# Input powers before the rotation tables and later in the block order; a fourth pooling block on unscaled input

## The chip, the cores and the metric

The kernel runs on one core of one Trainium2 chip. The core has five engines with queues of their own: TensorE (PE, matrix products into PSUM), VectorE (DVE), ScalarE (ACT), GpSimd (POOL) and SyncE (SP, which here issues nearly all DMAs). Each queue runs in order. The metric is device time of one execution in microseconds, the median over runs: 940.18 us before the change (3 runs, 939.85 to 941.1).

## The reference

A trunk of two layers over 512 tokens of width 1024, float32. Each layer normalises its input (RMSNorm), forms one wide projection of it, runs three mixers on slices of that projection, merges them by sigmoid gates, projects the sum and adds it to the residual:

```python
h = rmsnorm(x, norm_g[l])
z = h @ w_in[l]
a_val, a_gate, b_val, b_gate, c_u, c_v, c_gate, gates = jnp.split(z, split_idx, axis=-1)
ya = s5_mixer(a_val, ...) * jax.nn.silu(a_gate)
yb = pool_mixer(b_val, pool_w[l], pool_scale[l]) * jax.nn.silu(b_gate)
yc = sgu_mixer(c_u, c_v, ...) * jax.nn.silu(c_gate)
proj = einsum('blkc,kcd->blkd', stack([ya, yb, yc], 2), w_branch[l])
x = x + sum(sigmoid(gates) * proj, axis=2) @ w_out[l]
```

The s5 mixer is a diagonal complex state space: 32 groups of 16 channels with 64 states each, discretised from `lam`, `log_dt`, `b`, `c`, scanned over time, followed by GELU and a half GLU. The pool mixer takes, in four groups of channels (g = 0 to 3), the mean over a trailing window of 2, 4, 8 or 16 tokens minus the token, and maps each group by a 128x128 matrix. The third mixer (sgu) mixes positions in blocks of 128.

## The kernel before

**Blocks.** The work is a stream of blocks, each one product of a 1024x128 (or 512x128) piece of a weight matrix with the 512 tokens. Each weight and each activation is split into a rounded high part and a rest (`hi`/`lo`, `wh`/`wl`), and a step k of a product is three matmuls, hi x hi, lo x hi and hi x lo (`step`, lines 105 to 107). A block has 8 steps, a branch projection 4. SP loads the raw weights into three buffers `wr`, ACT makes `wh` (L157) and DVE makes `wl` (L158), each of three buffers, up to two blocks ahead of PE (`stream`; up to five are loaded or prepared).

**Layer 0, in PE's order.** Four value blocks for the state space, four pooling blocks (g = 3, 2, 1, 0), four pool gates (same order; each ends with a one-step product `psb` of the pooled group `pt[g]` with its split 128x128 matrix `wq[0]`), then the first merge: gate blocks `opened(m)` of 8 steps, and `joined(m)` of 4. Then the third mixer, its merge, the gates and GLU of the state space, its merge, and the output projection. Blocks before the norm is known run on the unscaled split input (`norm.hs`, tiles `gh`/`gl`) and are scaled afterwards by DVE (L739 for pooling). From the fourth value block on, `scaled()` makes the scaled input: per k a product `hf` on DVE (L675), `hi` on ACT (L677) and `lo` on DVE (L678). In `early` are the pooling groups of layer 0 that use the unscaled input: 3, 2 and 1; group 0 uses the scaled one, and ACT copies its result (L741).

**Side work.** The state space of a layer runs beside the blocks as a generator (`s5_side`). A software clock advances by 0.64 per step; in the fourth step of each product and at the end of each block a tick resumes the generator if its pause has passed. That decides where its PE instructions stand in PE's order, which is written out by hand. The order of the other engines is found by a planner at build time from its own estimate of durations; side work has lower priority there by 1000. Buffers of a pool are handed out in that planning too.

In layer 0 the generator first collects the values (`uu`), copies tables (`stacked`, on ACT), and writes `rotations`: some 150 small operations on POOL that build the tables `tlo` and `thi` from cos and sin of the discretisation. After a pause `W_POWERS` it writes `input_powers`: six DVE operations (L385, L386, L388) that make `ak` from `kre`, `kim`, `apr`, `api`, four transposes on PE (L391, `psa`), a copy on ACT (L393) and a store to DRAM (L394, `akd`). Then come four steps t: `s5_output`, `s5_input` (loads of `akd`, L457, and `bi`, L458, into buffers) and `s5_tables` (POOL, L501 to 507, from `tlo` and `thi`); after a pause (`W_PREP` for t = 0, else `W_OPS`) the lag products `psk` (L514); after `W_STATE` the state products `pse` (L550), whose results DVE multiplies with the tables at L555; after `W_OUT` the output products `psy` (L578 and L581), then GELU, a store and a gather into `ych` (L592). `outputs()` splits `ych` ahead of the GLU.

**Buffers.** `slot` is the large pool, 49 tiles of 128x512 (line 59). `spare` is a pool of six such tiles (`fp`, line 60) that the state space uses for `apr` and `api` (held until `stacked` and the powers have read them), `ai`, `bi`, `e`, `sbc` and others. `small_spare` is a pool of eight half tiles (`fs`, line 61) that holds the temporaries of the discretisation, of `rotations` (`tb`, L410) and of `input_powers` (`ak`, L384 and L387).

Of the kernel before, what the change touches and what calls it, by code (L numbers as in the profile page):

```python
# [7 lines left out]
F32 = mybir.dt.float32  # L8
# [7 lines left out]
P = 128  # L16
# [3 lines left out]
NS = 8  # L20
NK = 64
# [4 lines left out]
GELU_A = 0.044715  # L26
GELU_B = 1.5957691216057308
SIDE = 1000
W_POWERS = 32.0
W_PREP = (30.0, 25.0)  # L30
W_OPS = 15.0
W_STATE = 5.0
W_OUT = 16.0
# [19 lines left out]
def hybrid_trunk(ctx: ExitStack, tc, xT, wi, wbr, wo, wglu, wmisc, pv, rows, gain, slam, sbc, sbt, cst, out):  # L53
# [19 lines left out]
    def nm(s):  # L73
        count[0] += 1
        return f"{s}_{count[0]}"

    def slot(s="s", dt=F32, shape=(P, T)):
        return sp.tile(list(shape), dt, tag="s", name=nm(s))

    def spare(s="f", dt=F32, shape=(P, T)):  # L80
        return fp.tile(list(shape), dt, tag="f", name=nm(s))

    def small_spare(s="f", shape=(P, T // 2)):
        return fs.tile(list(shape), F32, tag="fs", name=nm(s))
# [282 lines left out]
    def stacked():  # L367
        for h in range(2):
            for r in range(2):
                a, b = slice(64 * r, 64 * r + 64), slice(64 * h, 64 * h + 64)  # L370
                for o, x, sign in ((war, apr, 1 - 2 * r), (wai, api, -1)):
                    S.activation(o[a].rearrange("p j (q h) -> p j h q", h=2)[:, :, h], x[b], AF.Copy, scale=float(sign))
                for o, x, sign in ((kar, kre, 1), (kai, kim, 2 * r - 1)):
                    S.activation(o[a].rearrange("p (q h) -> p h q", h=2)[:, h], x[b], AF.Copy, scale=float(sign))
# [63 lines left out]
    def flat(a):  # L438
        return a.rearrange("p q k -> p (q k)")
# [85 lines left out]
    def s5_side(l, ud, st):  # L525
        uu = bp.tile([P, 4, 8, NK], F32, tag="ba", name=nm("uu"))
        for s in range(NS):
            r = 16 * (NS - 1 - s)
            src = ud.rearrange("n (g c) (s k) -> s c (n g) k", c=16, s=NS)[s]
            nc.sync.dma_start(uu[r : r + 16].rearrange("p n g k -> p (n g) k"), src)  # L530
        if l == 0:
            stacked()
            rotations(*angle)
            yield W_POWERS
            input_powers()
            yield 3
        ych = bp.tile([P, 4, T], F32, tag="bb", name=nm("ych"))
        st["ych"] = ych
        for t in range(4):
            w = s5_output(l, t)  # L540
            e = s5_input(l, t)
            tcs, tsn, rt = s5_tables(l, t)
            yield W_PREP[l] if t == 0 else W_OPS
            s5_lags(l, t, w)
            yield W_STATE
            ps = pe.tile([P, 2, 4, NK], F32, tag="pe", name=nm("pse"))
            for r in range(2):
                for i in range(4):
                    for h in range(2):
                        PE.matmul(ps[64 * h : 64 * h + 64, r, i], e[r][:, 2 * i + h], uu[:, t, 2 * i + h], start=True, stop=True)  # L550
            sr, si = flat(ps[:, 0]), flat(ps[:, 1])

            def mul(x, y, eng=V):
                o = small_spare("p5")
                eng.tensor_tensor(o, x, y, ALU.mult)  # L555
                return o

            a, b = mul(sr, tcs), mul(si, tsn)
            G.tensor_tensor(a, a, b, ALU.add)  # L559
            d, c = mul(si, tcs), mul(sr, tsn)  # L560
            V.tensor_tensor(d, d, c, ALU.subtract)
            gr, gi = small_spare("g5"), small_spare("g5")
            V.tensor_tensor_scan(gr, rt, a, 0.0, ALU.mult, ALU.add)
            V.tensor_tensor_scan(gi, rt, d, 0.0, ALU.mult, ALU.add)
            b, c = mul(gi, tsn, G), mul(gr, tsn, G)
            a, d = mul(gr, tcs), mul(gi, tcs)
            v3 = lambda z: z.rearrange("p (q k) -> p q k", q=4)[:, :, 0 : NK - 1]
            for r, (x, y, op) in enumerate(((a, b, ALU.subtract), (d, c, ALU.add))):
                for h in range(2):
                    o = hst[64 * r : 64 * r + 64].rearrange("p (q h) k -> p h q k", h=2)[:, h, :, 1:NK]  # L570
                    i = slice(64 * h, 64 * h + 64)
                    V.tensor_tensor(o, v3(x)[i], v3(y)[i], op)
            yield W_OUT
            py = aux("psy")
            for g in range(8):
                for h in range(2):
                    o = py[64 * h : 64 * h + 64, g * NK : (g + 1) * NK]
                    PE.matmul(o, tm[:, g, 64 * h : 64 * h + 64], uu[:, t, g], start=True, stop=False)  # L578
                for h in range(2):
                    o = py[64 * h : 64 * h + 64, g * NK : (g + 1) * NK]  # L580
                    PE.matmul(o, w[:, g, 16 + 64 * h : 80 + 64 * h], hst[:, g], start=False, stop=True)  # L581
            sq = spare("sq")
            S.activation(sq, py, AF.Square)
            V.tensor_scalar(sq, sq, GELU_A, 1.0, ALU.mult, ALU.add)
            V.tensor_tensor(sq, sq, py, ALU.mult)
            S.activation(sq, sq, AF.Sigmoid, scale=GELU_B)
            V.tensor_tensor(sq, py, sq, ALU.mult)
            yd = dp.tile([P, T], F32, tag="yd", name=nm("yd"))
            nc.sync.dma_start(yd, sq)
            for g in range(8):  # L590
                src = yd.rearrange("(s c) (g k) -> g c s k", c=16, g=8)[g]
                nc.sync.dma_start(ych[16 * g : 16 * g + 16, t].rearrange("p (s k) -> p s k", s=NS), src)  # L592
# [45 lines left out]
    def layer(l, norm, nxt):  # L638
# [29 lines left out]
        def scaled():  # L668
            norm.spread()
            for n, ps in held:  # L670
                value(n, ps)
            held.clear()
            for k in range(8):
                t = slot("hf")
                V.scalar_tensor_tensor(t, xs[k], pcol(0, k), norm.rstd, ALU.mult, ALU.mult)  # L675
                hi, lo = slot("hi", F32R), slot("lo", F32R)
                S.activation(hi, t, AF.Copy)  # L677
                V.tensor_tensor(lo, t, hi.bitcast(F32), ALU.subtract)  # L678
                hs.append((hi, lo))
# [40 lines left out]
        wq = {}  # L720

        def small(i):
            raw = slot("wq", F32, (P, 4, P))
            nc.sync.dma_start(raw, wmisc[l, i])
            if i == 1:
                V.memset(raw[64:128, :, 0:64], 0.0)
            wq[i] = raw if i else split(raw, (P, 4, P))

        early = (3, 2, 1) if l == 0 else (3,)
        pt = [None] * 4  # L730
        yb = [None] * 4

        def pooled(g):
            def consume(ps):
                xp = bp.tile([P, NS, PAD + NK], F32, tag="xp", bufs=2, name=nm("xp"))
                G.memset(xp[:, :, 0:PAD], 0.0)
                xv = xp[:, :, PAD:].rearrange("p s (b k) -> p s b k", b=8)
                if g in early:
                    V.tensor_tensor(xv, by_block(ps), by_block(norm.rstd), ALU.mult)  # L739
                else:  # L740
                    S.activation(xv, by_block(ps), AF.Copy)  # L741
                cur = xp
                for j in range(g + 1):
                    nx = bp.tile([P, NS, PAD + NK], F32, tag="xq", bufs=2, name=nm("xq"))
                    if j < g:
                        G.memset(nx[:, :, 0:PAD], 0.0)
                    sh = 1 << j
                    if sh < NS:
                        G.tensor_tensor(nx[:, sh:NS, PAD:], cur[:, sh:NS, PAD:], cur[:, 0 : NS - sh, PAD:], ALU.add)
                        G.tensor_tensor(nx[:, 0:sh, PAD:], cur[:, 0:sh, PAD:], cur[:, NS - sh : NS, PAD - 1 : PAD - 1 + NK], ALU.add)  # L750
                    else:
                        o = PAD - sh // NS
                        G.tensor_tensor(nx[:, :, PAD:], cur[:, :, PAD:], cur[:, :, o : o + NK], ALU.add)
                    cur = nx
                t = slot("pt", F32, (P, NS, NK))
                V.scalar_tensor_tensor(t, cur[:, :, PAD:], 1.0 / (2 << g), xp[:, :, PAD:], ALU.mult, ALU.subtract)
                V.tensor_tensor(cur[:, :, PAD : PAD + 2], cur[:, :, PAD : PAD + 2], rcnt[:, g], ALU.mult)
                V.tensor_tensor(t[:, :, 0:2], cur[:, :, PAD : PAD + 2], xp[:, :, PAD : PAD + 2], ALU.subtract)
                pt[g] = split_steps(flat(t))
                if g == 3:  # L760
                    small(0)

            return consume
# [395 lines left out]
```

## Time and profile before

| | us |
|---|---|
| median of 3 runs | 940.18 |
| profiled execution | 941.43 |
| its span | 939.6 |
| PE busy | 882.9 (94%) |
| DVE busy | 578.1 (62%) |
| ACT busy | 299.9 (32%) |
| POOL busy | 216.0 (23%) |
| chain that ended last | PE 86%, DVE 6%, POOL 3%, DMA 2% |

The rows below are from one profiled execution. Times are from the start of its span. A wait names the operation whose end released the waiting one. Busy time of PE counts a matmul from its start to its modelled end. PEclk is the share of PE's clock that was granted; it has two levels, 1.2 and 2.4 GHz, and a value between them is a mean over a window.

### The profile page before, as it was taken

What the parts mean: (1) busy time and instruction counts of PE and PEld (TensorE: products, weight loads), DVE (VectorE), ACT (ScalarE), POOL (GpSimd) and SP (SyncE); (2) the same over time, 40 slices, a digit from 0 to 9 for tenths busy, and PEclk for the clock granted to TensorE, in tenths of its full rate; (3) what the DMA queues carried; (4) which work ended last, traced back from release to release, by engine and by line L of the source; (5) the groups of instructions that cost most, each with busy time, mean ns of one, the idle gap of its engine ahead of it and who ended that gap; (6) DMA issues with size and microseconds to landing.
All of it is one profiled execution on the core that took longest, in us unless ns stands there. A gap on an engine that the chain in (4) does not pass through costs nothing.

```text
span 939.6 us, 12276 instructions
## 1 busy us (share of the span) xinstructions
PE 882.9 (94%) x4652; PEld 719.5 (77%) x4652; DVE 578.1 (62%) x934; ACT 299.9 (32%) x440; POOL 216.0 (23%) x353
## 2 busy tenths in 40 slices
PE   9981199999999999999999999999999999999996
PEld 5861188888788878888888788887888888888885
DVE  8895173578867767444546787647884435544632
ACT  5334022322322225333433333231322223433521
POOL 1446940203233330000131730201321111000020
PEclk9986599999999999999999999999999999999998
DMA  7831033363425344223323824454432332322402
GB/s 241 168 103 45 12 90 105 121 197 119 133 80 160 92 145 146 78 92 112 112 92 135 144 72 132 142 167 140 140 101 90 92 110 82 109 91 91 156 23 89
DMA packets 65706, 106.89 MB, mean 114 GB/s; under 512 B 30176, under 2 KB 32864, under 8 KB 65648
## 3 DMA queue, kind: packets, MB, share of 16 engines
q1 hardware_dynamic: 65008, 104.88, 37.7%
q0 software_dynamic: 352, 1.10, 0.4%
q8 instruction: 36, 0.59, 0.3%
q14 instruction: 22, 0.18, 0.1%
q10 hardware_dynamic: 288, 0.14, 0.0%
HBM read 99.01 MB, written 7.08 MB: 113 GB/s over the span
## 4 chain that ended last, share of the span: by engine, by line
PE 86%; DVE 6%; POOL 3%; DMA 2%; issue 2%; ACT 1%; SPq 0%; DVEq 0%; ACTq 0%
PE mm L105 24%; PE mm L106 24%; PE mm L107 24%; PE mm L1024 2%; PE mm L1025 2%; PE mm L1026 2%; PE mm L843 1%; PE mm L844 1%; PE mm L845 1%; DVE wl L158 1%; POOL k L233 1%; PE pse L550 1%; DVE hf L675 1%; PE psy L578 1%; PE psz L865 1%
## 5 line engine op out<-in xcount | busy, mean ns | idle before, releaser
L105 PE MATMUL mm<-hi,wh 128*128 128x512 f32 x960 | 380.3, 396 | 2.8 <-ACT hi L677 2.8
L106 PE MATMUL mm<-lo,wh 128*128 128x512 f32 x960 | 376.7, 392 | 1.5 <-DVE lo L678 1.4
L107 PE MATMUL mm<-hi,wl 128*128 128x512 f32 x960 | 375.6, 391 | 1.3 <-DVE wl L158 1.3
L157 ACT ACTIVATE wh<-wr 128x1024 fp32r<-128x1024 f32 (+1 forms) x174 | 160.3, 922 | 448.5 <-PE mm L106 274.2
L158 DVE TENSOR_TENSOR wl<-wr,wh 128x1024 fp32r<-128x1024 f32 (+1 forms) x174 | 198.4, 1141 | 159.8 <-ACT wh L157 159.2
L105 PEld LDWEIGHTS mm<-hi,wh 128*128 128x128 f32 x960 | 181.5, 189 | 44.3 <-ACT hi L677 4.5
L106 PEld LDWEIGHTS mm<-lo,wh 128*128 128x128 f32 x960 | 181.5, 189 | 40.7 <-DVE lo L678 3.3
L107 PEld LDWEIGHTS mm<-hi,wl 128*128 128x128 f32 x960 | 181.5, 189 | 39.7 <-DVE wl L158 1.7
L799 DVE TENSOR_TENSOR sg<-sg,mm 128x512 f32<-128x512 f32 x48 | 32.8, 684 | 41.9 <-PE mm L107 41.9
L801 POOL TENSOR_TENSOR sg<-sg,sg 128x512 f32<-128x512 f32 x16 | 26.3, 1643 | 101.1 <-DVE sg L799 101.1
L614 POOL TENSOR_TENSOR sq<-sq,sq 128x512 f32<-128x512 f32 x7 | 12.7, 1813 | 125.0 <-ACT sq L608 114.1
L105 PE MATMUL mm<-gh,wh 128*128 128x512 f32 x96 | 38.4, 400 | 0.1
L107 PE MATMUL mm<-gh,wl 128*128 128x512 f32 x96 | 37.8, 393 | 0.4 <-DVE wl L163 0.4
L106 PE MATMUL mm<-gl,wh 128*128 128x512 f32 x96 | 37.7, 393 | 0.2 <-DVE gl L604 0.2
L391 PE MATMUL psa<-cs,ak 128*128 128x128 f32 x4 | 1.4, 447 | 38.8 <-DVE ak L388 38.8
L559 POOL TENSOR_TENSOR p<-p,p 128x256 f32<-128x256 f32 x8 | 5.9, 736 | 125.8 <-DVE p L555 125.8
L391 PEld LDWEIGHTS psa<-cs,ak 128*128 128x128 f32 x4 | 0.6, 202 | 39.6 <-DVE ak L388 39.6
L95 ACT ACTIVATE hi<-sg 128x512 fp32r<-128x512 f32 x32 | 20.2, 631 | 24.4 <-DVE sg L801 13.5
L790 ACT ACTIVATE sg<-mm 128x512 f32<-128x512 f32 x48 | 27.9, 581 | 0.0
L843 PE MATMUL mm<-wh,hi 128*128 128x512 f32 x64 | 25.4, 397 | 1.2 <-DVE sg L799 1.2
L844 PE MATMUL mm<-wl,hi 128*128 128x512 f32 x64 | 25.1, 392 | 0.9 <-DVE wl L158 0.9
L96 DVE TENSOR_TENSOR lo<-sg,hi 128x512 fp32r<-128x512 f32 x32 | 22.2, 695 | 5.9 <-ACT hi L95 5.7
(207 smaller groups left out, 1035.9 us busy)
## 6 DMA issues: line engine op xcount, KB each, us to landing
wr<-in_wi SPq DMA_DIRECT2D x102, 512.0 KB
wr<-in_wbr SPq DMA_DIRECT2D x48, 256.0 KB
wr<-in_wo SPq DMA_DIRECT2D x16, 512.0 KB
ai<-akd SPq DMA_DIRECT2D x16, 256.0 KB
bi<-in_sbt SPq DMA_DIRECT2D x16, 256.0 KB
x<-in_xT SPq DMA_DIRECT2D x8, 256.0 KB
ud<-u SPq DMA_DIRECT2D x8, 256.0 KB
uu<-ud SPq DMA_DIRECT2D x16, 128.0 KB
```

The costliest lines, as they stand in the source:

```text
L95: S.activation(hi, src, AF.Copy)
L96: V.tensor_tensor(lo, src, hi.bitcast(F32), ALU.subtract)
L105: PE.matmul(ps, whi[:, k], x[0], start=k == 0, stop=False)
L106: PE.matmul(ps, whi[:, k], x[1], start=False, stop=False)
L107: PE.matmul(ps, wlo[:, k], x[0], start=False, stop=k == n - 1)
L157: S.activation(hi, raw, AF.Copy)
L158: V.tensor_tensor(lo, raw, hi.bitcast(F32), ALU.subtract)
L790: S.activation(sg[m], ps, AF.Sigmoid)
L799: V.tensor_tensor(g, g, ps, ALU.mult)
L801: (V if last is not None else G).tensor_tensor(g, g, macc[m], ALU.add)
L843: PE.matmul(ps, th, w(wh), start=j == 0 and k == 0, stop=False)
L844: PE.matmul(ps, th, w(wl), start=False, stop=False)
```

## The change

Five edits. In `s5_side` of layer 0 the pause `W_POWERS` now comes ahead of `stacked`, `input_powers` and `rotations`, is 50 in place of 32, and the powers are written ahead of the tables. The pause before the lag products of step 0 is 25 in place of 30 in layer 0 (25 in layer 1, as before). `hf` (both layers) and `pt` are taken from the six spares in place of the large pool, and so is the raw tile of the pooling weights. The pooling block of group 0 in layer 0 runs on the unscaled input and is scaled by DVE.

```diff
--- before.py
+++ after.py
@@ -26,8 +26,8 @@
 GELU_A = 0.044715
 GELU_B = 1.5957691216057308
 SIDE = 1000
-W_POWERS = 32.0
-W_PREP = (30.0, 25.0)
+W_POWERS = 50.0
+W_PREP = (25.0, 25.0)
 W_OPS = 15.0
 W_STATE = 5.0
 W_OUT = 16.0
@@ -529,10 +529,10 @@
             src = ud.rearrange("n (g c) (s k) -> s c (n g) k", c=16, s=NS)[s]
             nc.sync.dma_start(uu[r : r + 16].rearrange("p n g k -> p (n g) k"), src)
         if l == 0:
+            yield W_POWERS
             stacked()
+            input_powers()
             rotations(*angle)
-            yield W_POWERS
-            input_powers()
             yield 3
         ych = bp.tile([P, 4, T], F32, tag="bb", name=nm("ych"))
         st["ych"] = ych
@@ -671,7 +671,7 @@
                 value(n, ps)
             held.clear()
             for k in range(8):
-                t = slot("hf")
+                t = spare("hf")
                 V.scalar_tensor_tensor(t, xs[k], pcol(0, k), norm.rstd, ALU.mult, ALU.mult)
                 hi, lo = slot("hi", F32R), slot("lo", F32R)
                 S.activation(hi, t, AF.Copy)
@@ -720,13 +720,13 @@
         wq = {}
 
         def small(i):
-            raw = slot("wq", F32, (P, 4, P))
+            raw = slot("wq", F32, (P, 4, P)) if i else spare("wq", F32, (P, 4, P))
             nc.sync.dma_start(raw, wmisc[l, i])
             if i == 1:
                 V.memset(raw[64:128, :, 0:64], 0.0)
             wq[i] = raw if i else split(raw, (P, 4, P))
 
-        early = (3, 2, 1) if l == 0 else (3,)
+        early = (3, 2, 1, 0) if l == 0 else (3,)
         pt = [None] * 4
         yb = [None] * 4
 
@@ -752,7 +752,7 @@
                         o = PAD - sh // NS
                         G.tensor_tensor(nx[:, :, PAD:], cur[:, :, PAD:], cur[:, :, o : o + NK], ALU.add)
                     cur = nx
-                t = slot("pt", F32, (P, NS, NK))
+                t = spare("pt", F32, (P, NS, NK))
                 V.scalar_tensor_tensor(t, cur[:, :, PAD:], 1.0 / (2 << g), xp[:, :, PAD:], ALU.mult, ALU.subtract)
                 V.tensor_tensor(cur[:, :, PAD : PAD + 2], cur[:, :, PAD : PAD + 2], rcnt[:, g], ALU.mult)
                 V.tensor_tensor(t[:, :, 0:2], cur[:, :, PAD : PAD + 2], xp[:, :, PAD : PAD + 2], ALU.subtract)
```

## Rows read from the trace of the kernel before

**Rows 1.** The page, part 1: busy us, share of the span, instructions

```profile
PE 882.9 (94%) x4652; PEld 719.5 (77%) x4652; DVE 578.1 (62%) x934; ACT 299.9 (32%) x440; POOL 216.0 (23%) x353
```

**Rows 2.** Waits of PE, 0 to 120 us: total us, times, longest

```profile
PE psa L391 <- DVE ak L388: 38.8, 2, 38.2
...
PE mm L105 <- ACT hi L677: 1.8, 3, 0.6
```

**Rows 3.** Timeline of PE: start, us, engine, line, operation, [idle before <- releaser]

```profile
48.77 0.39 PE L105 MATMUL mm<-hi,wh 128*128 128x512 f32 x1
...
67.35 0.39 PE L105 MATMUL psb<-hi,hi 128*128 128x512 f32 x1
...
73.47 0.39 PE L105 MATMUL psb<-hi,hi 128*128 128x512 f32 x1
...
113.76 0.69 PE L391 MATMUL psa<-cs,ak 128*128 128x128 f32 x2 [0.54 <-DVE ak L388]
...
114.10 0.78 PE L105 MATMUL mm<-hi,wh 128*128 128x512 f32 x1
...
119.21 0.40 PE L105 MATMUL mm<-hi,wh 128*128 128x512 f32 x1
```

**Rows 4.** Windows: length, busy of PE, PEld, DVE, ACT, POOL; PEclk, DMA, GB/s

```profile
53.00:64.40 11.40, 8.94 (x21) 5.74 (x22) 11.18 (x29) 4.55 (x7) 4.62 (x8) 0.70 0.40 135
...
112.00:119.20 7.20, 6.13 (x16) 4.63 (x17) 4.12 (x9) 1.02 (x2) 6.79 (x20) 0.51 0.15 43
```

**Rows 5.** Timeline of DVE, around the powers

```profile
65.46 0.68 DVE L96 TENSOR_TENSOR lo<-wq,hi 128x512 fp32r<-128x512 f32 x1
...
80.71 0.23 DVE L364 TENSOR_TENSOR kim<-k,inv 128x32 f32<-128x32 f32 x1
...
110.96 0.53 DVE L385 TENSOR_TENSOR ak<-kre,apr 128x256 f32<-128x256 f32 x1 [22.03 <-POOL thi L413]
```

**Rows 6.** Windows, the stretch of the last pooling block and two gates

```profile
48.77:74.20 25.43, 22.58 (x79) 16.17 (x77) 25.04 (x71) 8.93 (x13) 10.47 (x18) 0.87 0.28 94
```

**Rows 7.** Timeline of POOL, the rotation tables

```profile
77.81 0.93 POOL L233 TENSOR_TENSOR k<-k 128x32 f32<-128x32 f32 x2
...
90.90 0.26 POOL L411 TENSOR_TENSOR tb<-tlo,k 128x32 f32<-128x32 f32 x1
...
125.63 1.88 POOL L503 TENSOR_TENSOR tp<-tp,tp 128x256 f32<-128x256 f32 x2
```

**Rows 8.** Windows: POOL's tables in all, and one group of them twice

```profile
77.81:127.51 49.70, 14.44 (x53) 11.47 (x54) 17.64 (x37) 10.51 (x25) 46.27 (x159) 0.59 0.14 43
...
98.61:103.86 5.25, 0.00 (x0) 0.00 (x0) 0.00 (x0) 0.00 (x0) 4.92 (x18) 0.50 0.00 0
...
113.42:120.82 7.40, 7.06 (x21) 5.66 (x22) 4.35 (x10) 1.02 (x2) 7.07 (x19) 0.62 0.31 76
```

**Rows 9.** Timeline of DVE, state step 0

```profile
163.63 1.42 DVE L555 TENSOR_TENSOR p<-pse,tp 128x256 f32<-128x256 f32 x4 [1.79 <-PE pse L550]
...
167.99 1.22 DVE L158 TENSOR_TENSOR wl<-wr,wh 128x512 fp32r<-128x512 f32 x1
```

**Rows 10.** Timeline of DVE, first and last of the 16 that prepare step 0

```profile
113.62 0.34 DVE L478 TENSOR_TENSOR bt<-sbc,kar 128x128 f32<-128x128 f32 x1
...
131.59 0.68 DVE L467 TENSOR_TENSOR bi<-bi,bi 128x512 f32<-128x512 f32 x1
```

**Rows 11.** Timelines of PE, SP and ACT, end of step 3 in layer 0

```profile
325.51 0.34 PE L578 MATMUL psy<-uu,tm 128*64 128x64 f32 x4
...
339.69 0.43 SPq L592 DMA_DIRECT2D ych<-yd  x1
...
362.40 0.67 ACT L932 ACTIVATE sg<-mm,pvt 128x512 f32<-128x512 f32 x1
```

**Rows 12.** Waits of SP's issue queue: total us, times, longest

```profile
SPq L394 <- ACT ak L393: 37.1, 1, 37.1
...
SPq L457 <- DVE bpad L481: 13.0, 3, 4.5
```

## The prediction

> **What bounds the kernel now.** I read the page's busy times first: TensorE (PE) is busy for 882.9 of 939.6 us, so outside its own work only some 57 us can be won [rows 1]. The waits of PE in the first 120 us say where most of that lies: 38.8 us at line 391, the transposes of the input powers `ak`, and 1.8 us on `hi`, the scaled input [rows 2]. The timeline of PE gives their places. Three matmuls, one step k, take 0.68 us there: the nine steps between the two pool-gate products at 67.35 and 73.47 take 6.12. The second product ends at 73.47 + 0.68 = 74.15, and the next block starts at 114.10 [rows 3]. The granted clock says that a wait costs more than itself: after the 38 us it was 0.51 of full speed, the lower level of 1.2 GHz, until 119.2, and after the short waits on `hi` the stretch from 53.0 to 64.4 had 0.70 [rows 4].
>
> Why `ak` was late stands on VectorE (DVE) and GpSimd (POOL). `kim`, the last input of the powers, was done at 80.94. The first `ak` started at 110.96, after 22.03 us of idleness that ended with POOL's `thi` at line 413 [rows 5]. It reads nothing of `thi`: it needs a buffer of the small pool, eight of them, which the rotation tables, written ahead of it in the program, were passing through. POOL worked on those tables from 77.81, and on what is built from them until 127.51 [rows 7]. So a DVE job of 2.8 us (110.96 to the last transposes at 113.76) stood behind POOL's long chain of small operations. That is the wait that ends last in this stage.
>
> **The change part by part.**
> *The powers ahead of the tables.* The six `ak` operations now take their buffers first; DVE can run them when `kim` is there. No work is added. The PE position moves as well: by the block clock (0.64 per step) the first pause of 50 ends at the tick in the second gate block of the first merge, instead of behind the second pool gate. Between the two lie pool gate 1 (9 steps), pool gate 0 (9), one gate block (8) and half of another (4): 30 x 0.68 = 20.4 us of PE work that now come first. Gone is the wait, 114.10 - 74.15 = 39.95 us, less 0.25 for the four transposes themselves, and the half clock behind it: the twelve matmuls from 114.10 to 119.21 took 5.1 us where 12 x 0.227 = 2.7 is usual. A = 39.7 + 2.4 = 42.1 us.
>
> *The fourth pooling block on unscaled input.* Scaled input is then first wanted by the pool gates, one block of 8 x 0.68 = 5.44 us later. From 48.77, where the last pooling block starts, to 67.35 there are 16 steps, 10.88 us; it took 18.58. B is at most 18.58 - 10.88 = 7.7 us, waits and clock together. It is nothing if DVE doesn't get ahead: from 48.8 to 74.2 DVE was busy for 25.0 of 25.4 us [rows 6], and the low half of the pooling weights was ready at 65.46 + 0.68 = 66.14 for a product at 67.35, 1.2 us of margin [rows 3, 5]. A PE that comes 7.7 us earlier meets that. For a gain speaks that the eight `hf`, the four `pt` and the raw pooling weights no longer queue for the buffers which the unscaled input holds, so the planner may load and split the weights sooner. Added is one DVE operation of 0.7 us in place of one on ScalarE. I take B = 4, the middle of 0 to 7.7.
>
> *Where `ak` is then late.* PE would reach the transposes at 74.15 - 4 + 20.4 = 90.5 us. DVE had `kim` at 80.94; to this come the `ak` at 2.8, the weight split of 1.2 for the block that PE now runs on, and up to three gates' products and splits at some 2.0 each (three operations of 0.68), 6: 90.9. Lower bound 0 (DVE orders the powers first), upper bound 8 us (B full, PE there at 86.9, all of DVE's rest in front, and the half clock behind the wait). I take C = 1.5, near the 90.9. On SyncE the store of `akd` held the weight loads queued behind it for 37.1 us of issue time [rows 12]; that shrinks with the wait.
>
> *The tables and the shorter pauses.* This is what the old wait hid. Step 0 of the state space now starts 30 steps later on PE, but its first matmuls on the state come sooner behind the transposes: 35.84 on the block clock instead of 42.24. 35.84 x 0.68 / 0.64 = 38.1, with 1.5 for the small matmuls: DVE reaches line 555 at about 92 + 39.5 = 131.5 and needs POOL's tables there. Before, they were done at 127.51 and line 555 started at 163.63, 36 us of margin [rows 7, 9]. POOL slows beside DVE: the same group of table work took 5.25 us with DVE idle and 7.40 with DVE busy for 4.35 of them, a loss of half of DVE's time [rows 8]. The 17.64 us of DVE time in POOL's 49.70 cost 8.7, so alone it is 41.0. After the change DVE has, from 78 to 131, some 26 us of operations with both inputs in SBUF: weight splits 6 x 1.2 and 5 x 0.68 (10.6), `ak` 2.8, the preparation of step 0 (16 operations, 113.62 to 132.27, some 10) [rows 10], gate splits 2.7. At half, 13 us: tables at 77.8 + 41 + 13 = 131.8, level with DVE. The chain of 4.4 us behind line 555, until the next weight split at 167.99 [rows 9], passed before without a wait of PE; with two blocks prepared ahead, 8 us less the split itself, 1.6 us of wait on DVE are free. I take D = 1 for a start of the tables a little late, bounds 0 and 14 (R1).
>
> The Trainium skill (SBUF — State Buffer, Who interferes with whom) has a harsher rule: between GpSimd and a VectorE operation with two SBUF inputs the shared port is an exclusive lock, and the loser blocks fully. By it the group in rows 8 would have taken 5.25 + 4.35 = 9.6 us; the trace shows 7.40. By the rule POOL alone needs 32.1 and the 26 us count whole: tables at 136, PE 5 us later in place of 1, in all 901.
>
> *The end of step 3.* The last output product of layer 0 moves by 240.64 - 230.40 = 10.24 on the block clock, 10.9 us. Before, it started at 325.51, its last gather was issued by 340.12 (14.6 later), and the first GLU result was read at 362.40, so that block of 2.7 us started at 359.7 [rows 11]. 325.5 + 10.9 + 14.6, up to 4 for the gather to land and 1.3 to split: 356.3 against 359.7. Cost 0, upper bound 3.
>
> The sum: 42.1 + 4 - 1.5 - 1 = 43.6 us. The profiled execution took 941.43 us (span 939.6 and 1.8 around it), the median is 940.18, 1.25 lower. 941.43 - 43.6 - 1.25 = 896.6, so 897.
>
> **The rivals.**
> R1, the tables take the place of the powers. If POOL starts them only when PE has transposed the powers (two of the eight buffers stay taken until then, and POOL works in order), they are done at 90.5 + 41 + 13 = 144.5; DVE waits 13, PE 11.4 and 2.4 of clock instead of 1: 897 + 13 = 910. A start halfway gives 903 to 904. For it: POOL's chain is real, and the planner that put `ak` in front of 22 us of idleness thought it short. Against: its first 13 us (77.8 to the first `tb`) need no such buffer.
> R2, DVE keeps the stage: B = 0 and C = 8 give 42.1 - 8 - 1 = 33.1, 907. For it: DVE without a gap. Against: gates 1 and 0 need not stand in front of the powers.
> R3, the change does not do what it says: `ak` still gets buffers that the tables pass through. It is done at 113.7 as before, or 5 later with POOL slowed by more DVE work. PE waits 23 to 28 us from 90.5, and 2.4 of clock: 42.1 + 4 less 25.4 to 30.4 is a gain of 16 to 21: 919 to 924. Against: the written order is reversed.
> R4, slower than before: the spares run short. `hf`, `pt` and the raw weights join the state space in six spare buffers, of which two are held by the state powers until the powers are made. SyncE's loads into spares (`ai`, `bi`) then wait in front of the weight loads. Such waits were 13.0 us over three, the longest 4.5 [rows 12]. Four blocks are loaded or prepared ahead, 16 us in a merge at 4.1 each, so only what exceeds 16 us counts, at each of eight state steps: slower than before from a wait of 16 + 43.6 / 8 = 21.5 us on; at 22.5 it is 897 + 52 = 949. Five times the longest wait seen.
>
> **How the numbers follow.** Forecast 0.54, R1 0.22, R2 0.12, R3 0.08, R4 0.04. The forecast's own range is 890 (A + B in full, no C and D: 49.8) to 903. R1 up to a late start and R2 take it to 914; R3 and R4 are left out. About 0.2% can be told from no change here. Faster 0.95: all but R4 and a remnant; same 0.01, slower 0.04.
>
> **What would show it.** Right: the wait at line 391 is under 3 us and the transposes run near 90 us; `ak` starts within 10 us of `kim` and waits for no POOL operation; the pooling and gate blocks run at full clock from 48 us on; line 555 of step 0 waits for POOL for less than 4 us. Wrong: DVE idle for 10 us or more in front of line 555 (R1); PE waiting on `hi`, `lo` or the operands of `psb` between 54 and 90 (R2); `ak` released by line 413 again (R3); SyncE waiting long at lines 457 or 724 (R4).

## The result: 904.35 us, and the profile after

The changed kernel takes 904.35 us (median, 903.62 to 904.57) against 940.01 us of the kernel before, run beside it: a ratio of 0.962, 95% interval 0.9603 to 0.9637. The forecast was 897 in a range of 890 to 914. The profiled execution has a span of 902.7 us against 939.6, so 36.9 us went, where the sum said 43.6.

The page after, part 1, to be read beside [rows 1]: TensorE (PE) does the same work in 37 us less time.

```profile
PE 880.1 (97%) x4652; PEld 719.6 (80%) x4652; DVE 571.8 (63%) x935; ACT 299.6 (33%) x439; POOL 234.9 (26%) x353
```

Waits of PE in the kernel after, 0 to 120 us (us in total, times, longest), which answer to [rows 2]: of the 38.8 us at line 391 there are 5.5 left, and the waits on `hi` are gone.

```profile
PE psa L391 <- DVE ak L388: 5.5, 2, 3.4
```

The timeline of PE after [rows 3]. The first pool-gate product starts at 59.83, not 67.35. The transposes come in two pairs with a wait of 2.10 and one of 3.42, and the twelve matmuls behind them take 5.0 us, most of them 0.43 us apart where 0.23 is usual. Then, in layer 1, a wait that the kernel before did not have, on the split of the pooling weights (line 95), and again matmuls 0.43 us apart.

```profile
59.83 0.39 PE L105 MATMUL psb<-hi,hi 128*128 128x512 f32 x1
...
89.29 0.44 PE L391 MATMUL psa<-cs,ak 128*128 128x128 f32 x2 [2.10 <-DVE ak L388]
93.14 0.69 PE L391 MATMUL psa<-cs,ak 128*128 128x128 f32 x2 [3.42 <-DVE ak L388]
93.48 0.78 PE L105 MATMUL mm<-hi,wh 128*128 128x512 f32 x1
...
503.93 0.52 PE L105 MATMUL psb<-hi,hi 128*128 128x512 f32 x1 [4.45 <-ACT hi L95]
```

Windows of the kernel after (columns as in [rows 4]). The stretch 53.0 to 64.4 has the full clock now (it had 0.70), DVE is still without a gap until 78.2, and there are two places at the lower level: behind the transposes and behind the new wait in layer 1.

```profile
53.00:64.40 11.40, 11.40 (x52) 9.42 (x51) 11.30 (x30) 3.42 (x5) 7.52 (x12) 1.00 0.33 111
48.77:78.20 29.43, 29.43 (x132) 24.36 (x131) 29.14 (x78) 10.11 (x15) 14.15 (x22) 1.00 0.37 110
90.00:95.00 5.00, 1.86 (x6) 1.57 (x7) 2.26 (x3) 3.93 (x9) 4.51 (x14) 0.63 0.00 0
95.00:100.00 5.00, 5.00 (x17) 4.01 (x16) 2.28 (x4) 1.12 (x2) 4.84 (x16) 0.69 0.50 160
504.00:512.00 8.00, 7.80 (x32) 5.16 (x33) 6.32 (x9) 2.09 (x4) 7.74 (x12) 0.57 0.30 99
78.22:138.37 60.15, 54.63 (x271) 44.11 (x270) 37.20 (x83) 21.65 (x42) 56.25 (x152) 0.94 0.33 99
```

The same places of PE in both timelines make a ledger:

| PE starts | before | after | ahead by |
|---|---|---|---|
| first pool-gate product, layer 0 | 67.35 | 59.83 | 7.5 |
| first product of layer 1 (`ps`) | 495.17 | 453.91 | 41.3 |
| first pool-gate product, layer 1 | 542.68 | 503.93 | 38.8 |
| second pool-gate product, layer 1 | 549.64 | 514.59 | 35.1 |
| last output product of step 3, layer 1 | 715.02 | 678.12 | 36.9 |
| end of the span | 939.6 | 902.7 | 36.9 |

So layer 0 brought nearly what the sum said, layer 1 lost 6.2 us up to its second pool gate, and 1.9 came back later.

**Layer 0.** The timeline of DVE after [rows 5, 9, 10]. The first `ak` follows `kim` at once and waits for nothing of GpSimd (POOL), but `kim` itself is 6.5 us later than before. The last `ak` stands behind a `lo` of a gate, and that waited for a `hi` on ScalarE (ACT). Further on `bt` (line 478) waits for POOL's `thi`, and line 555 for its `tp`, about one us.

```profile
87.18 0.27 DVE L364 TENSOR_TENSOR kim<-k,inv 128x32 f32<-128x32 f32 x1
87.37 0.41 DVE L385 TENSOR_TENSOR ak<-kre,apr 128x256 f32<-128x256 f32 x1
...
92.00 0.69 DVE L96 TENSOR_TENSOR lo<-y,hi 128x512 fp32r<-128x512 f32 x1 [2.01 <-ACT hi L95]
92.61 0.47 DVE L388 TENSOR_TENSOR ak<-ak,ak 128x256 f32<-128x256 f32 x1
...
123.35 0.39 DVE L478 TENSOR_TENSOR bt<-sbc,kar 128x128 f32<-128x128 f32 x1 [3.47 <-POOL thi L413]
...
137.77 0.42 DVE L555 TENSOR_TENSOR p<-pse,tp 128x256 f32<-128x256 f32 x1 [0.83 <-POOL tp L503]
```

The timeline of ACT after shows what that `hi` stood behind: the copies of `stacked`. They wait for `apr`, `kre` and `kim`, and so ran some 6 us earlier before.

```profile
85.59 0.96 ACT L374 ACTIVATE kar<-kre 64x32 f32<-64x32 f32 x4 [0.79 <-DVE kre L363]
86.56 1.89 ACT L372 ACTIVATE war<-apr 64x288 f32<-64x288 f32 x4
88.47 1.88 ACT L372 ACTIVATE wai<-api 64x288 f32<-64x288 f32 x4
90.36 0.96 ACT L374 ACTIVATE kai<-kim 64x32 f32<-64x32 f32 x4
91.34 0.63 ACT L95 ACTIVATE hi<-y 128x512 fp32r<-128x512 f32 x1
```

In the kernel before, a `lo` of a gate waited for such a `hi` too, but no power stood behind it (its timeline of DVE):

```profile
85.22 0.75 DVE L96 TENSOR_TENSOR lo<-y,hi 128x512 fp32r<-128x512 f32 x1 [3.62 <-ACT hi L95]
```

The timeline of POOL after [rows 7]: the tables start at about the same time and end at 138.4 in place of 127.5.

```profile
78.22 0.50 POOL L233 TENSOR_TENSOR k<-k 128x32 f32<-128x32 f32 x2 [7.81 <-DVE k L233]
...
95.51 0.26 POOL L411 TENSOR_TENSOR tb<-tlo,k 128x32 f32<-128x32 f32 x1
...
137.00 1.43 POOL L503 TENSOR_TENSOR tp<-tp,tp 128x256 f32<-128x256 f32 x2
```

**Layer 1.** Two DVE rows after, from the place that lost. Six `hf` run in a row: they hold all six spares. Later an operation of the state space stands 7.91 us waiting for a load of `bi`, with the pooling product `pt` behind it.

```profile
461.27 4.06 DVE L675 SCALAR_TENSOR_TENSOR hf<-x,pvt,rstd 128x512 f32<-128x512 f32 x6
...
498.64 0.69 DVE L463 TENSOR_TENSOR m<-ai,bi 128x512 f32<-128x512 f32 x1 [7.91 <-DMA bi<-in_sbt]
```

SyncE's (SP's) timeline after, the same stretch: the loads for state step 0 of layer 1, which the kernel before issued in layer 0 (first fence, from its timeline of SP), now come from 469 on, around the gather of `uu` (second fence), and the pooling weights (line 724) are loaded at 500.76 for a product that PE could have started at 499.5. The third fence is SP's own wait ahead of that load [rows 12].

```profile
330.43 0.62 SPq L457 DMA_DIRECT2D ai<-akd  x1
...
332.09 0.43 SPq L458 DMA_DIRECT2D bi<-in_sbt  x1
```

```profile
468.90 0.33 SPq L472 DMA_DIRECT2D sbc<-in_sbc  x1
...
480.83 6.89 SPq L530 DMA_DIRECT2D uu<-ud  x7
...
489.40 0.89 SPq L458 DMA_DIRECT2D bi<-in_sbt  x1
...
500.76 0.33 SPq L724 DMA_DIRECT2D wq<-in_wmisc  x1
```

```profile
SPq L724 <- DVE e L464: 8.6, 1, 8.6
```

### The profile page after: what moved, and what is told of

Same layout as the page of the kernel before. It is cut to its first block, busy times and chain, and to the rows that moved or that the text cites. A ratio compares the mean times of both kernels' runs of the same rounds, so it can differ in the third digit from the quotient of the medians.

```text
span 902.7 us, 12286 instructions
## 1 busy us (share of the span) xinstructions
PE 880.1 (97%) x4652; PEld 719.6 (80%) x4652; DVE 571.8 (63%) x935; ACT 299.6 (33%) x439; POOL 234.9 (26%) x353
## 4 chain that ended last, share of the span: by engine, by line
PE 82%; DVE 8%; DMA 5%; issue 2%; SPq 1%; ACT 1%; DVEq 0%; POOL 0%
PE mm L105 24%; PE mm L106 23%; PE mm L107 23%; DVE wl L158 2%; PE mm L1024 2%; PE mm L1025 2%; PE mm L1026 2%; DMA ai<-akd 1%; DMA bi<-in_sbt 1%; DMA sbc<-in_sbc 1%; PE pse L550 1%; PE psz L865 1%; DMA wr<-in_wi 1%; SPq L530 1%; PE mm L1020 1%
## 5 line engine op out<-in xcount | busy, mean ns | idle before, releaser
L105 PE MATMUL mm<-hi,wh 128*128 128x512 f32 x952 | 376.2, 395 | 0.0
L106 PE MATMUL mm<-lo,wh 128*128 128x512 f32 x952 | 372.3, 391 | 0.0
L158 DVE TENSOR_TENSOR wl<-wr,wh 128x1024 fp32r<-128x1024 f32 (+1 forms) x174 | 195.2, 1122 | 149.3 <-ACT wh L157 149.0
L799 DVE TENSOR_TENSOR sg<-sg,mm 128x512 f32<-128x512 f32 x48 | 32.9, 685 | 40.6 <-PE mm L107 40.5
L614 POOL TENSOR_TENSOR sq<-sq,sq 128x512 f32<-128x512 f32 x7 | 12.7, 1812 | 129.9 <-ACT sq L608 119.0
L106 PE MATMUL mm<-gl,wh 128*128 128x512 f32 x104 | 40.8, 393 | 0.6 <-DVE gl L604 0.6
L105 PE MATMUL mm<-gh,wh 128*128 128x512 f32 x104 | 41.3, 397 | 0.1
L107 PE MATMUL mm<-gh,wl 128*128 128x512 f32 x104 | 40.9, 393 | 0.4 <-DVE wl L163 0.4
L875 POOL TENSOR_TENSOR sg<-sg,z 128x512 f32<-128x512 f32 x8 | 15.8, 1972 | 45.4 <-DVE z L867 45.4
L843 PE MATMUL mm<-wh,hi 128*128 128x512 f32 x64 | 25.4, 396 | 0.7 <-DVE sg L799 0.7
L1024 PE MATMUL mm<-wh,hi 128*128 128x512 f32 x64 | 25.3, 396 | 0.0
L844 PE MATMUL mm<-wl,hi 128*128 128x512 f32 x64 | 25.0, 390 | 0.0
L1025 PE MATMUL mm<-wl,hi 128*128 128x512 f32 x64 | 24.9, 390 | 0.0
```

Of the source, the lines that this page charges most:

```text
L105: PE.matmul(ps, whi[:, k], x[0], start=k == 0, stop=False)
L106: PE.matmul(ps, whi[:, k], x[1], start=False, stop=False)
L107: PE.matmul(ps, wlo[:, k], x[0], start=False, stop=k == n - 1)
L158: V.tensor_tensor(lo, raw, hi.bitcast(F32), ALU.subtract)
L799: V.tensor_tensor(g, g, ps, ALU.mult)
L843: PE.matmul(ps, th, w(wh), start=j == 0 and k == 0, stop=False)
```

## The experiments

Diffs are against the changed kernel unless said. Ratios are to the kernel before on the same chip (941.2 to 942.0 us there).

**Where layer 1 lost: `hf` in the large pool again, layer 1 only.**

```diff
-                t = spare("hf")
+                t = slot("hf") if l else spare("hf")
```

> The changed kernel, with the eight hf of layer 1 back in the large pool (layer 0 as changed). Theory A: in layer 1 the hf fill the six spares, so the preparation of state step 0 (its loads ai and bi and 16 DVE operations), which before was done in layer 0 at 334 to 354 us, runs beside the pooling blocks instead; DVE waits 7.9 us for bi there and PE 4.5 us plus half clock at the first pool gate, some 6 us in all. Then this kernel does the preparation in layer 0 again and takes 904.35 - 6 = 898 (897 to 900). Theory B: the late raw pooling weights alone (issued at 500.8 when a spare came free) hold PE; hf has no part: 904 (903 to 905), the wait at the first pool gate of layer 1 stays at 4 us or more.

900.13 us, ratio 0.9546 (0.9523 to 0.9569), 0.1 above A's 897 to 900. The wait of 4.5 us is gone; the waits of PE between 450 and 540 us in that kernel:

```profile
PE mm L105 <- ACT hi L677: 1.0, 1, 1.0
PE mm L106 <- DVE lo L678: 0.4, 1, 0.4
```

The timeline of SP in that kernel: the loads of step 0 are back in layer 0, and the pooling weights are loaded 19 us sooner.

```profile
303.65 0.60 SPq L457 DMA_DIRECT2D ai<-akd  x1
...
305.19 0.33 SPq L458 DMA_DIRECT2D bi<-in_sbt  x1
...
481.71 0.43 SPq L724 DMA_DIRECT2D wq<-in_wmisc  x1
```

Theory A holds: `hf` in the spares pushed step 0's preparation into layer 1's busiest stretch. The size is 4.2 us beside a kernel with the order of the changed one on the same chip (904.31, the one after the next), and 3.6 in the spans, where A said 6.

**The rival: the pooling weights' own buffer.**

```diff
-            raw = slot("wq", F32, (P, 4, P)) if i else spare("wq", F32, (P, 4, P))
+            raw = slot("wq", F32, (P, 4, P)) if i or l else spare("wq", F32, (P, 4, P))
```

> The changed kernel, with only the raw pooling weights of layer 1 back in the large pool. Theory B (the raw weights wait for a spare): the load is issued some 10 us earlier, the first pool gate of layer 1 does not wait, 898 (897 to 900). Theory A (the preparation of step 0 in the wrong place): DVE still waits 7.9 us for bi with the pooled group 3 queued behind it, whose low half came at 504.5, so PE waits for that instead: 904 (903 to 905).

908.61 us, ratio 0.9641 (0.9617 to 0.9665): not faster, but 4.3 us slower than the 904.31 of the same chip, which neither theory said. The waits of PE between 450 and 540 us, in that kernel:

```profile
PE psb L105 <- ACT hi L95: 4.1, 1, 4.1
PE psb L107 <- DVE lo L96: 3.2, 1, 3.2
```

Theory B falls: with a buffer of its own the load still stood behind `bi` in SP's queue (issued at 491.71), and DVE still waited 7.6 us for `bi`. Why the two waits of PE add up to more here (7.3 us in place of 4.5) was not tried.

**The wait left at line 391: `stacked` written last.**

```diff
-            stacked()
             input_powers()
             rotations(*angle)
+            stacked()
```

> The changed kernel, with the 16 table copies on ACT (stacked) written behind the powers and the rotation tables. Theory C: these copies stand in front of a gate split on ACT, DVE waits 2.0 us for that split with the last ak behind it, and PE 3.4 us at the second pair of transposes. Without them there the last ak is done near 90.5 in place of 93.1, the wait at line 391 goes from 5.5 to about 3.2 us: 902 (900.5 to 903), less if the half clock behind the wait goes as well. Rival D: DVE's own backlog sets the last ak, another operation takes the place of that wait: 904 (903.3 to 905).

904.31 us, ratio 0.9593 (0.9575 to 0.9611), the wait again 5.5 us. The planner put the copies where they were; the written order changed nothing on ACT, so this run says nothing of theory C.

**What the written order alone brings (against the kernel before).**

```diff
             stacked()
-            rotations(*angle)
             yield W_POWERS
             input_powers()
+            rotations(*angle)
```

> The kernel before, with the rotation tables written behind the powers and nothing else changed (first pause 32, pooling group 0 on scaled input, temporaries in the large pool). Theory E: the wait of 38.8 us came from the buffers that the tables pass through; PE still reaches the transposes at 74 us, the powers are done at 84 to 88, PE waits 10 to 14 us, all else about as before: 940 less 26 to 30, 912 (909 to 917). Rival F: the tables hold the powers whatever the order, only the later place on PE helped: 938 to 941.

915.94 us, ratio 0.9706 (0.9674 to 0.9738): 942.0 x 0.0294 = 27.7 us of the changed kernel's 36. The transposes stay early in PE's order and wait 9.7 us for DVE, not 38.8 [rows 2]. Theory E holds: the wait was for a buffer, and the order in the program decides who has it first.

**The tables first, at the later place in PE's order.**

```diff
-            yield W_POWERS
             stacked()
-            input_powers()
             rotations(*angle)
+            yield W_POWERS
+            input_powers()
```

> The changed kernel with the two jobs in the old order (copies and rotation tables written before the pause of 50, the powers behind it). Theory E (the powers are bound to the tables' buffers): PE reaches the transposes at 87 us as now, the powers come at 113 to 118, PE waits 26 to 31 us there; 904.35 + 20 to 25: 924 to 930. Rival F (the later place on PE is what counted): 903 to 908.

927.35 us, ratio 0.984 (0.981 to 0.9869). The timeline of DVE there has the old wait, though PE asks 13 us later (87.0 in place of 74.15):

```profile
114.30 0.52 DVE L385 TENSOR_TENSOR ak<-kre,apr 128x256 f32<-128x256 f32 x1 [20.27 <-POOL thi L413]
```

Theory E again, and close to the price of R3 (919 to 924 forecast): `ak` is done at 117.0, wherever PE asks for it.

**Is it the unscaled group 0 that brings the pool gates forward?**

```diff
-        early = (3, 2, 1, 0) if l == 0 else (3,)
+        early = (3, 2, 1) if l == 0 else (3,)
```

> The changed kernel with pooling group 0 on scaled input again. The changed kernel reached the first pool-gate product 7.5 us earlier than the one before, and then lost 8.5 us at the transposes (6.2 us of wait, 2.3 of half clock). Theory G: the two are one account, DVE's powers set the time of the transposes whenever PE is early; without the earlier arrival PE comes at about 94 us and waits for nothing: 904.35 + 7.5 - 8.5 = 903 (901 to 906). Rival H: the fourth block on unscaled input is worth its 7.5 us by itself (DVE's powers come later too when PE is later): 910 to 912.

905.41 us, ratio 0.9617 (0.9595 to 0.9638), the same as the changed kernel (0.962). And the first pool-gate product is where it was:

```profile
59.65 0.39 PE L105 MATMUL psb<-hi,hi 128*128 128x512 f32 x1
```

So rival H falls, and term B does not come from the unscaled block. G's number is met, but not by G's mechanism, since PE came no later. Nor does B come from the written order: that product starts at 66.96 with the order alone changed, and at 59.68 with the tables written first. What is left of the edits for it is the buffers of `hf`, `pt` and `wq`, or the pauses (neither run alone). The wait at line 391 was 2.7 us there, with no half clock behind it, and that too was worth nothing at the end: `bt` then waited 9.3 us for `thi`, and PE 1.5 us at `psk` for what is made from it and 1.9 for `wh` and `wl` on the way to `psy`.

**`stacked` held back behind the copy of the transposes** (which `input_powers` returns for it).

```diff
-            stacked()
-            input_powers()
+            copied = input_powers()
+            with tc.issue_after(copied): stacked()
```

> The changed kernel, with the 16 table copies on ACT held behind the copy of the transposed powers (writing them later did not move them: the planner puts them where their inputs are ready). Theory C: DVE no longer waits 2.0 us for the gate split on ACT, the last ak is done at about 90.8 in place of 93.1, the wait at line 391 goes from 5.5 to about 3.2 us; with the half clock unchanged 902, with less of it 900: 900 to 902.5. Rival D: DVE's backlog or the copies' own users (the tables of step 0) give it back: 904 to 905.

904.5 us, ratio 0.962 (0.9592 to 0.9647): D's number. The wait at 391 falls from 5.5 to 3.5 and step 0's `psk` starts 3.3 us sooner (125.13 against 128.46), but nothing is left of it at the end. PE loses it after `pse` of step 0: 1.2 us waiting for `wl` ahead of `psy`, then 2.1 at `pse` of step 1 for `e` and `bi` (1.3 in the changed kernel) with a granted clock of 0.66 from 181 to 186. DVE there:

```profile
123.46 0.39 DVE L478 TENSOR_TENSOR bt<-sbc,kar 128x128 f32<-128x128 f32 x1 [7.00 <-POOL thi L413]
```

`bt` starts at 123.5 whether DVE is ready 3.5 or 7 us before. PE does not wait for it here; whether DVE's lost 7 us made the later operands late is not shown.

**The `hf` edit with a longer pause (54), so that PE asks still later.**

```diff
-W_POWERS = 50.0
+W_POWERS = 54.0
```

> The changed kernel with hf of layer 1 in the large pool and the first pause 54 in place of 50: the transposes stand 8 steps (5.4 us) later on PE, all of the state space in layer 0 some 5 us later. Theory C: the 8.5 us lost at the transposes go but for 1: 900.1 - 7.5 = 892.5 (891 to 895) in the measure of the run with hf alone. Rival I: the end of step 3 comes too late for the GLU of layer 0 (15 us for a chain of 19): PE waits 3 to 6 us there: 895 to 899.

903.01 us, ratio 0.9592 (0.9568 to 0.9615): slower than the `hf` edit alone, though the transposes (95.05) wait for nothing. From `psk` to `pse` PE takes 11.1 us in place of 6.3. Two operations wait for `thi` there, `bt` on DVE and `rt` (line 506) on ACT, and the weights that PE waits for are the `wh` behind `rt` (timelines of DVE, ACT and PE):

```profile
123.08 0.39 DVE L478 TENSOR_TENSOR bt<-sbc,kar 128x128 f32<-128x128 f32 x1 [8.89 <-POOL thi L413]
130.48 0.41 ACT L506 ACTIVATE rt<-rho 128x256 f32<-128x256 f32 x1 [12.09 <-POOL thi L413]
131.89 0.78 PE L105 MATMUL mm<-hi,wh 128*128 128x512 f32 x1 [2.98 <-ACT wh L157]
```

Rival I shows as well: PE waits 2.8 us for the `lo` of `ych` in the GLU of layer 0 (waits of PE, 300 to 340 us), where the kernel with the `hf` edit alone has no such wait. The number, 903, is above both theories.

```profile
PE mm L106 <- DVE lo L435: 2.8, 3, 1.8
```

**Are the small buffers what holds step 0? `bt` out of them.** Three kernels, each with the `hf` edit and this one:

```diff
-        p0, p1 = (small_spare("bt", (P, 4, 2, 16)) for _ in range(2))
+        p0, p1 = ((slot("bt", F32, (P, 4, 2, 16)) if l + t == 0 else small_spare("bt", (P, 4, 2, 16))) for _ in range(2))
```

> The changed kernel with hf from the large pool in layer 1 and the two temporaries bt of the first state step (L478, L479) from the large pool in place of the small buffers, which the rotation tables hold until 123.5 us. Theory T (small buffers hold step 0): DVE no longer waits 3.5 us for thi at L478, bt runs at about 118 to 120; PE's psk stays at 128.8, since no wait of PE stood there, so the time stays with the kernel that has only the hf edit (900.1), 898 to 901. Rival U (the planner reorders DVE and the split wl comes late): 902 to 905, with a wait of PE for wl or wh between 118 and 130 us.

899.69 us, ratio 0.955 (0.9528 to 0.9572); `bt` runs at 100.1 without a wait. As theory T said, no gain, since PE did not wait there.

> The same with the stacked copies behind the copy of psa as well. Theory T: psa waits 3.5 us in place of 5.5, psk at 125.1, bt at L478 without a wait for thi (it was 7.0), so the 3.3 us are kept at step 0: pse at 131.4 without a wait, and 895.5 to 899 in all. Rival V (the tables themselves, not their buffers, are the next bound): L555 waits for tp until about 138, some 4 to 6 us, PE waits for its results ahead of psy, and the time is 899.5 to 903.

898.8 us, ratio 0.9551 (0.9527 to 0.9576): inside T's numbers, but no better than the kernel without the held-back copies. `psk` starts at 125.17, 2.3 us before the last kernel's, and of that 0.7 is left at `psy` (153.39 against 154.06). The tables' end is not what takes it: line 555 waits 1.3 us in both. ACT waits 9.95 us for `thi` there (line 506) and PE 1.0 us for a `wl` and 0.8 at `pse` of step 1; that this is what took it was not tried in this pair. Inconclusive between T and V.

> The same as the first with the pause ahead of the powers 54 in place of 50. psa (about 95.0) waits for nothing, as without the bt edit. Theory T: the 8.9 us wait of DVE at L478 goes, wl is no longer late behind it, psk to pse takes 6.3 us again in place of 11.1, and the time falls from 903.0 to 896 to 899. Rival V: the wait moves to L555 for tp and the time stays at 901 to 904.

903.88 us, ratio 0.9593 (0.9573 to 0.9614): V's number, not by V's mechanism. Line 555 waits for no table, and `bt` runs at 103.5 without a wait; but the wait that PE pays for was on ACT already (12.09 us in the kernel without this edit) and is still there, at `rt`, which needs a small buffer too, with the split `wh` behind it:

```profile
130.50 0.41 ACT L506 ACTIVATE rt<-rho 128x256 f32<-128x256 f32 x1 [11.76 <-POOL thi L413]
130.82 1.56 ACT L157 ACTIVATE wh<-wr 128x1024 fp32r<-128x1024 f32 x2
```

and PE pays for it (its timeline), 12.7 us from `psk` to `pse`:

```profile
128.61 0.64 PE L514 MATMUL psk<-w,bpad 128*32 128x128 f32 x16
131.91 0.50 PE L105 MATMUL mm<-hi,wh 128*128 128x512 f32 x1 [2.66 <-ACT wh L157]
...
141.29 0.69 PE L550 MATMUL pse<-uu,e 128*64 128x64 f32 x16
```

**And `rt` out of them too** (on top of the last kernel).

```diff
-        rt = small_spare("rt", (P, 4, NK))
+        rt = slot("rt", F32, (P, 4, NK)) if l + t == 0 else small_spare("rt", (P, 4, NK))
```

> The kernel with hf (layer 1) and bt (first state step) from the large pool and the pause 54, with the table rt of the first state step (L506, ACT) from the large pool as well. With bt moved alone the wait had not gone: it moved to ACT's rt at L506, 11.8 us for thi, with the split wh queued behind it, PE waited 2.7 us for wh and psk to pse took 12.7 us. Theory T (the small buffers that the tables hold stop each later user in turn): ACT doesn't wait at L506, PE doesn't wait between psk (128.6) and pse, which comes 6.3 us after it (134.9), L555 waits 2 to 4 us for tp, and the time falls from 903.9 to 896.5 to 899.5. Rival V (the tables' own end on POOL, about 137, is the bound): the wait moves on to tp at L555 and PE loses as much as before, first psy again at 160 to 162, 902 to 905.

899.77 us, ratio 0.9549 (0.9528 to 0.957), 4.1 us below the last. `rt` runs at 104.5, the waits of PE on `wh` and `wl` between 80 and 150 us are gone (those on `hi` and `lo` of a gate, 2.3 us, stay), and `pse` follows `psk` by 6.3 us. Line 555 waits 0.3 us for `tp`, less than T said. Theory T holds for step 0, with a time 0.3 above its range. That time is still no better than with the `hf` edit alone: the powers stand 8 steps (5.4 us) later on PE and wait for nothing, but PE pays at the GLU, as rival I of the pause 54 said, with 2.7 us of wait and a granted clock of 0.79 from 314 to 322 (waits of PE, 300 to 340 us):

```profile
PE mm L106 <- DVE lo L435: 2.7, 2, 1.9
```

The `hf` edit alone (0.9546) and the three with 0.9549 to 0.9551 can't be told apart; all four beat both kernels, and the one-line `hf` edit is the one to keep.

## Why the prediction was right, and where it was not

The forecast's mechanism is what happened, and 904.35 lies in its range. It also lies nearer to R2's 907 than to 897, but not by R2, which had B at 0: between 48 and 87 us PE waited for no `hi`, `lo` or `psb` operand. R2's C of 8 did come.

**A, 42.1: right.** `ak` waited for a buffer, not for data. With the order alone changed 27.7 us came; with the place changed and the order not, the 20 us wait for `thi` stayed.

**B, +4 of 0 to 7.7: in full, 7.5, and for another reason than its heading.** With group 0 on scaled input it came all the same. The buffers, which I had named only as speaking for a gain, are what is left, by elimination.

**C, -1.5 of 0 to 8: 8.5, past its upper bound.** PE is at the transposes at 78.19 + 13 x 0.68 = 87.0 and goes on at 93.48: 6.2 us beyond the four transposes, and 2.3 of half clock (twelve matmuls in 5.0 us for 2.7). The step that failed is that DVE "had `kim` at 80.94": I kept that time while letting PE run ahead. DVE had no gap, so a PE that is 7.5 us ahead puts its own splits and products in front, and `kim` was done at 87.45. The runs bear this out: `kim` was done at 81.5 with the order alone changed, where PE is not early, and at 87.3 with the tables first, where it is. B and C were one term: 7.5 - 8.5, about -1, where I had +2.5. The bound that I worked out for "B full" had PE there at 86.9; it needed to be the forecast once B was full. A smaller part, 2.0 us, was the ACT queue: the `stacked` copies ahead of a gate's `hi`, which I had costed nowhere. Their written place does not do it (written last, they ran at the same time); they follow `apr`, `kre` and `kim`, and came late with them. Kernels with less of this wait (2.7, 3.5 or none) gained nothing at the end. For the one with none, the small buffers took 4.1 us of that, and with them free PE still loses at a gate's `hi` ahead of the transposes (2.1 us) and at the GLU (2.7), each with half clock behind it; for the other two the cause is read from their traces and not tried.

**D, -1 of 0 to 14: the cost was right, its working was not.** Tables at 138.4, not 131.8. The rate holds roughly: POOL took 60.15 us beside 37.20 us of DVE work, and with the 41.0 us that I estimated for POOL alone that is a loss of 0.51 of DVE's time. But of these 37 us some 30 are operations with both inputs in SBUF, the kind that I had counted as 26 up to 131 and that the group in [rows 8] consists of; of them the loss is 0.64, beside 0.49 there. By the Trainium skill's exclusive lock (SBUF — State Buffer, Who interferes with whom) those 30 us would count whole wherever DVE has the port first; the trace shows a loss of 19 us. It cost PE nothing, by luck: C had made step 0 later as well, with `pse` at 134.74. Nor did I see that the tables hold step 0 by their buffers too, at `bt` and `rt`: R1's mechanism at other lines. In the changed kernel PE does not wait for it yet; with the pause 54 it cost 4.1 us.

**End of step 3, 0: right.** PE waits for nothing there.

Layer 0 by these sizes: 42.1 + 7.5 - 8.5 = 41.1, and the ledger has 41.3.

**What was not in the sum: layer 1, 6.2 us at the pool gates, 4.4 at the end.** This is R4's mechanism at a place that R4 did not name. I priced it by loads held in front of weight loads and dismissed it by the 16 us of blocks in store; but the diff takes `hf` from the spares "in both layers", and there eight `hf` meet the preparation of layer 1's step 0. Not a wait of 21 us but a reordering: the planner prepared step 0 in layer 1 itself, no longer a layer ahead. The sign that I had named, SP waiting at line 724, is there with 8.6 us. With the one-line edit the time is 0.9546 of before: 42.7 us less by the ratio and 40.5 in the spans (899.1 against 939.6), beside the 43.6 forecast. Part of that closeness is luck: B came 3.5 us above what the sum had and C 7.0 below. The order and the pause without the other edits were not run.

**Named signs.** Right: transposes near 90 us, `ak` behind `kim` without POOL, full clock from 48 us on, line 555 waiting 1.1 us. Wrong: the wait at 391 under 3 us (5.5).

## What to carry to other kernels

A wait whose releaser the operation does not read is a wait for a buffer: look for the pool, and ask who takes it first in the program; after the mend, ask which other operations draw on the same pool, for each can become the next wait. When an engine without gaps serves two streams, a gain of one stream is a delay of the other, so such terms are summed as one. A pool that a change begins to use in a loop over layers must be priced in each layer. A job that is moved later to spare a wait moves what follows it too: look at the end of its chain before counting the gain.

## What the chip showed that I had not expected

Short waits can cost half of their length again in the clock, and not always. Two waits of 5.5 us in all at 87 to 93 us were followed by a granted clock of 0.63 and 0.69 and 2.3 us of loss, and the 4.5 us at 503.93 by 0.57 until about 511. In the kernel with the pause 54 and `bt` moved, waits of 2.7 and 0.5 us behind the small matmuls of `psk` were followed by matmuls 0.43 us apart from 133.2 to 138.9 (a granted clock of 0.66 from 130 to 140), while the 2.2 us on a gate's `hi` near 92 us brought none (1.00 from 90 to 95). In the last kernel 2.1 us at that place came with these windows, so the same wait is priced either way:

```profile
90.00:95.00 5.00, 2.64 (x9) 1.57 (x8) 3.00 (x6) 4.91 (x12) 4.59 (x13) 0.89 0.00 0
95.00:100.00 5.00, 5.00 (x21) 4.03 (x20) 2.52 (x4) 1.60 (x3) 4.67 (x17) 0.77 0.59 210
```
